# One hybrid encoder kernel: weight chunks split two ahead, index lookups in three queued parts, attention in steps of two heads of each group

## The chip, the cores and the metric

The kernel runs on one core of a Trainium2 chip, in one launch. The metric is the time of the launch on the device in microseconds (us); less is better. Engines: PE (TensorE, matrix multiply), PEld (its weight loads), DVE (VectorE), ACT (ScalarE), POOL (GpSimd), SP (SyncE, which issues most DMAs). Each engine works through its own queue in order and waits there for what an instruction needs.

## What is computed

Two layers over 512 tokens of width 1024. Each layer has a mixer (attention in windows, a short convolution and a pooling branch side by side) and a PEER block, a retrieval of 16384 one-neuron experts. Cut to what matters:

```python
for l in range(2):
    h = rms_norm(x, norm1_g[l]) * (1 + scale1) + shift1
    q, k, v, conv_x, conv_b, conv_c, pool_x = split(h @ w_in[l])
    attn = windowed_gqa(rope(norm(q)), rope(norm(k)), v, sink)   # 8 q heads, 2 kv heads, blocks of 128, +-128 tokens
    conv = conv_b * short_conv(conv_c * conv_x)                  # 256 channels
    pool = per_group_map(multiscale_pool(pool_x)) * pool_scale   # 256 channels, windows 2, 4, 8, 16
    x = x + gate1 * (concat(attn, conv, pool) @ w_out[l])
    h2 = rms_norm(x, norm2_g[l]) * (1 + scale2) + shift2
    # PEER: two scores of 128 keys per head, top 16 of each, top 16 of their 256 sums
    v1, i1 = top_k(q1 @ keys0.T, 16); v2, i2 = top_k(q2 @ keys1.T, 16)
    top, pos = top_k(v1[:, None] + v2[None, :], 16)
    e = (i1 * 128 + i2)[pos]; gate = softmax(top)                # 8 heads x 16 experts a token
    x = x + gate2 * sum_k(gate_k * gelu(h2 . peer_u[e_k]) * peer_v[e_k])
```

## The kernel before

Activations lie transposed in SBUF, 128 features on the partitions and 512 tokens along the row (`hh` and `hl`, a high and a low part, since f32 products are built from three matmuls of parts).

**The weight stream.** All large weights (w_in, w_out, peer_wq and the transposed peer_u) come as chunks of 128 x 1024. A chunk is loaded into `wr` by a DMA that SP issues (L251), its high part is cast into `wh` by ScalarE (`prep_hi`, L263), and the low part is the difference, `wl`, made by DVE or GpSimd (`prep_lo`, L272). `half` lists chunks with the high part alone, `ready` those with both. `chunk` (L295) takes a ready one, prepares one high and one low part for later chunks, and then queues the 24 matmuls of its own (L291 to L293: high x high, high x low, low x high). There are three `wh` and three `wl` buffers and five `wr`. In the steady state one chunk is ready and one half.

**do_A** (L816) is one such chunk of peer_u against 384 of the 512 tokens, then a gelu on ScalarE (L822) and, for the first AHEAD = 56 of the 128 chunks, a DMA of the result to `Sd` in DRAM (L824). These 56 stand in as PE work beside the selection; the rest follow in the dense stage.

**The selection and slots.** `scores` and `pairs` run DVE's max, index and replace operations for the top 16. `slots` (L1178) turns positions of the top 16 sums into two indices and the gates, some twenty DVE operations. `lookup` (L1212) picks the expert indices by these: ScalarE copies the indices out into `rep` (L1216), DVE compares (`soh`, L1218), multiplies by `rep` (L1220) and adds up (L1223, L1226). `operands` transposes the results on PE (L930), and ScalarE and DVE lay them out as `ij` and `gg`.

**The token loop** (`g8`, 48 groups of 8 tokens): DVE makes one-hot matrices `oh` for the next group (L949 to L952), PE multiplies them (L980, L981) into a matrix of gates over experts, ScalarE copies it to `stg` (L983), and every fourth group goes to `Gd` in DRAM. At groups 3 and 7 of each 16 a `lookup` for the next 128 tokens is queued whole. `fill` keeps two sums, of DVE's and of PE's work in us, and queues a do_A whenever PE's lags, up to do_A 51; the others follow behind the loop.

**The dense stage** runs over 128 expert blocks: load of peer_v, high and low part (`vh`, `vl`), weights from `Gd` and the gelu, 18 matmuls (`vmul`, L1033 to L1038), and for the last 128 tokens gathers by indirect DMA with DVE products.

**Attention** runs in eight steps (four blocks of 128 queries, two kv groups `g`). `att_scores` does four heads of one group: one f32 matmul each on 64 rows of `qk` (L674, two passes), masks by bf16 matmuls on 128 rows (L678), row maximum on DVE (L681), then exponentials on ScalarE (L692). `att_norm` scales, `att_turn` transposes on PE (L712), `att_out` multiplies by `v` (L721). On PE a step is: transposes of step i, scores of step i + 2, output of step i.

The order on each engine is the order in which the program issues; tile pools with a fixed number of buffers add the waits.

## Time and profile before

| | us |
|---|---|
| median of 3 runs (3032.3 to 3038.93) | 3036.97 |
| the profiled execution | 3036.9 |
| its span, first to last instruction | 3035.1 |
| PE busy in the span | 2904.2 (96%) |
| DVE busy | 2401.6 (79%) |
| ACT busy | 1265.9 (42%) |
| POOL busy | 918.0 (30%) |
| mean granted clock of PE | 0.977 |

Busy times of engines overlap and don't add up to the span. A busy PE is not PE at its peak: ends of matmuls are modelled, and a matmul at the lower clock counts as busy for longer. So the rows below give idle time, clock and waits by stage.

### The profile page before, as it was taken

The numbers are of one execution on the slowest core, as the hardware profiler recorded it, in microseconds if no ns is written. First come the engines' busy times: TensorE is split into PE (matmuls) and PEld (weight loads), VectorE is DVE, ScalarE is ACT, GpSimd is POOL, SyncE is SP. The second block draws the span as 40 slices with busy tenths as digits, with TensorE's granted clock in tenths as the row PEclk, the third lists the DMA queues.
The fourth block names the chain that finished last, engine by engine and source line by source line (L and its number), as shares of the span: only waits on it lengthen the run. The fifth ranks groups of instructions, "written<-read, shape, count | busy, mean of one in ns | idle before, by whom it ended". The sixth has DMA issues, their size and how long they took to land.

```text
span 3035.1 us, 41249 instructions
## 1 busy us (share of the span) xinstructions
PE 2904.2 (96%) x15116; PEld 2507.1 (83%) x15116; DVE 2401.6 (79%) x4617; ACT 1265.9 (42%) x1774; POOL 918.0 (30%) x782
## 2 busy tenths in 40 slices
PE   5999979999999999999999999799999999999999
PEld 3647879889888888888866678798988888888887
DVE  7966978776888888888868579778578888888887
ACT  4343346664333333333343343566633333333332
POOL 5405500002343343333333243000033333334342
PEclk7999989999999999999999999899999999999999
DMA  6524236569999999999943323465799999999996
GB/s 229 174 71 133 87 101 239 211 224 331 349 359 354 350 366 350 347 361 355 328 146 125 104 80 97 133 234 213 263 324 337 332 350 337 330 342 350 326 336 236
DMA packets 312971, 782.73 MB, mean 258 GB/s; under 512 B 26784, under 2 KB 154176, under 8 KB 309696
## 3 DMA queue, kind: packets, MB, share of 16 engines
q1 hardware_dynamic: 218992, 438.68, 42.7%
q0 software_dynamic: 73920, 268.53, 24.1%
q10 hardware_dynamic: 19856, 72.88, 6.2%
q8 instruction: 118, 1.93, 0.3%
q14 instruction: 85, 0.70, 0.1%
HBM read 705.02 MB, written 74.97 MB: 257 GB/s over the span
## 4 chain that ended last, share of the span: by engine, by line
PE 81%; DVE 14%; ACT 3%; issue 1%; POOL 0%; ACTq 0%; DMA 0%; DVEq 0%; POOLq 0%
PE pa L293 13%; PE pa L291 13%; PE pa L292 13%; PE pb L1034 6%; PE pb L1035 6%; PE pb L1038 6%; PE pb L1033 6%; PE pb L1037 6%; PE pb L1036 6%; PE pb L980 1%; PE pb L981 1%; PE pb L721 1%; PE pb L674 1%; DVE wl L272 1%; DVE I L1163 1%
## 5 line engine op out<-in xcount | busy, mean ns | idle before, releaser
L293 PE MATMUL pa<-hh,wl 128*128 128x384 f32 (+1 forms) x2568 | 906.9, 353 | 64.3 <-DVE wl L272 64.3
L291 PE MATMUL pa<-hh,wh 128*128 128x384 f32 (+1 forms) x2568 | 915.9, 357 | 28.1 <-ACT hh L364 24.5
L292 PE MATMUL pa<-hl,wh 128*128 128x384 f32 (+1 forms) x2568 | 903.8, 352 | 10.2 <-DVE hl L357 9.7
L293 PEld LDWEIGHTS pa<-hh,wl 128*128 128x128 f32 x2568 | 493.2, 192 | 91.1 <-DVE wl L272 69.9
L291 PEld LDWEIGHTS pa<-hh,wh 128*128 128x128 f32 x2568 | 493.9, 192 | 71.1 <-ACT hh L364 26.8
L1015 DVE TENSOR_TENSOR vl<-vr,vh 128x1024 fp32r<-128x1024 f32 x256 | 313.7, 1225 | 291.4 <-ACT vh L1014 277.4
L292 PEld LDWEIGHTS pa<-hl,wh 128*128 128x128 f32 x2568 | 492.9, 192 | 39.9 <-DVE hl L357 14.0
L1014 ACT CAST vh<-vr 128x1024 fp32r<-128x1024 f32 x256 | 269.5, 1053 | 504.0 <-PE pb L1038 266.3
L1051 POOL DMA_INDIRECT row<-in_peer_u_dram,eidx x256 | 307.8, 1202 | 541.7 <-DVE acc L1064 406.9
L1060 POOL DMA_INDIRECT row<-in_peer_v_dram,eidx x256 | 311.2, 1216 | 458.3 <-DVE row L1055 408.4
L272 DVE TENSOR_TENSOR wl<-wr,wh 128x1024 fp32r<-128x1024 f32 x265 | 323.5, 1228 | 82.2 <-ACT wh L263 79.2
L263 ACT CAST wh<-wr 128x1024 fp32r<-128x1024 f32 x331 | 348.8, 1055 | 75.6 <-PE pa L292 32.5
L1064 DVE SCALAR_TENSOR_TENSOR acc<-row,gw,acc 128x1024 f32<-128x1024 f32 x256 | 327.6, 1280 | 0.1
L822 ACT ACTIVATE ga<-pa 128x384 f32<-128x384 f32 x256 | 125.8, 492 | 466.7 <-PE pa L293 464.5
L1055 DVE SCALAR_TENSOR_TENSOR row<-row,htok 128x1024 f32<-128x1024 f32 x256 | 311.8, 1219 | 0.0
L1034 PE MATMUL pb<-vh,whi 128*128 128x512 f32 x768 | 300.7, 392 | 0.0
L1035 PE MATMUL pb<-vl,whi 128*128 128x512 f32 x768 | 300.5, 391 | 0.0
L1038 PE MATMUL pb<-vh,wlo 128*128 128x512 f32 x768 | 299.9, 391 | 0.0
L1037 PE MATMUL pb<-vh,wlo 128*128 128x512 f32 x768 | 299.3, 390 | 0.0
L1033 PE MATMUL pb<-vh,whi 128*128 128x512 f32 x768 | 299.0, 389 | 0.0
L1036 PE MATMUL pb<-vl,whi 128*128 128x512 f32 x768 | 298.5, 389 | 0.0
L272 POOL TENSOR_TENSOR wl<-wr,wh 128x1024 fp32r<-128x1024 f32 x66 | 170.0, 2587 | 198.1 <-ACT wh L263 198.1
(304 smaller groups left out, 3820.8 us busy)
## 6 DMA issues: line engine op xcount, KB each, us to landing
wr<-in_peer_uT_dram SPq DMA_DIRECT2D x256, 512.0 KB
vr<-in_peer_v_dram SPq DMA_DIRECT2D x256, 512.0 KB
Gd<-stg ACTq DMA_DIRECT2D x24, 2048.0 KB
adaw<-in_w_ada_dram SPq DMA_DIRECT2D x80, 512.0 KB
gtFalse<-Gd SPq DMA_DIRECT2D x36, 768.0 KB
Sd<-ga ACTq DMA_DIRECT2D x112, 192.0 KB
gtTrue<-Gd SPq DMA_DIRECT2D x28, 768.0 KB
gs<-Sd SPq DMA_DIRECT2D x112, 192.0 KB
```

The source lines that it names most:

```text
L263: self.nc.scalar.copy(hi, raw)
L272: (eng or self.nc.vector).tensor_tensor(lo, raw, hi.bitcast(F32), ALU.subtract)
L291: nc.tensor.matmul(ps[:, :width], wh, hh[c][:, :width], start=c == first, stop=False)
L292: nc.tensor.matmul(ps[:, :width], wh, hl[c][:, :width], start=False, stop=False)
L293: nc.tensor.matmul(ps[:, :width], wl, hh[c][:, :width], start=False, stop=c == last)
L1033: nc.tensor.matmul(y0, a, vh[:, 0:512], start=f, stop=False)
L1034: nc.tensor.matmul(y1, a, vh[:, 512:1024], start=f, stop=False)
L1035: nc.tensor.matmul(y0, a, vl[:, 0:512], start=False, stop=False)
L1036: nc.tensor.matmul(y1, a, vl[:, 512:1024], start=False, stop=False)
L1037: nc.tensor.matmul(y0, z, vh[:, 0:512], start=False, stop=e)
L1038: nc.tensor.matmul(y1, z, vh[:, 512:1024], start=False, stop=e)
L1064: nc.vector.scalar_tensor_tensor(acc, r, wb[bt - 1][:, k:k + 1], acc, ALU.mult, ALU.add)
```

## The change

Five edits:

1. `stream_init` gets `deep = 1`; `do_A` sets it to 2 for the first 56 chunks, and `chunk` then goes on preparing until two chunks are ready. `wh` has four buffers.
2. The pool branch writes its mean into a tile that it already has and the difference into `u`, so the two `pm` tiles are gone.
3. Attention steps take two heads of each group: four score matmuls alternate between rows 0 to 63 and 64 to 127 and come before all masks; the output is two matmuls of 256 columns per key block, one for each group.
4. `slots` is a generator that stops before its last part; a do_A is queued there.
5. `lookup` is a generator of three parts: `rep` on ScalarE; compare and multiply; the adds. In the token loop they are queued at groups 2, 3, 4 and 6, 7, 8, and `fill` is told 2.5 and 1.8 us instead of 5.5. `operands` still stands at group 11.

```diff
--- before.py
+++ after.py
@@ -244,6 +244,7 @@
         self.raws = []
+        self.deep = 1
@@ -259,7 +260,7 @@
         if hi is None:
-            hi = self.wp.tile([P, D], F32R, tag="wh", name=self.n("wh"), bufs=3)
+            hi = self.wp.tile([P, D], F32R, tag="wh", name=self.n("wh"), bufs=4)
@@ -296,6 +297,9 @@
         self.prep_lo(eng)
+        while self.deep > len(self.ready) and self.half:
+            self.prep_hi()
+            self.prep_lo(eng)
@@ -559,18 +563,18 @@
                 g.tensor_tensor(s4[:, 2:527], s2[:, 1:526], s2[:, 3:528], ALU.add)
-                dst = t([P, S], F32, "pm", bufs=2)
-                if c == 0:
-                    g.tensor_tensor(dst[0:64], s2[0:64, 8:520], self.icnt[0:64, 0], ALU.mult)
-                    g.tensor_tensor(dst[64:128], s4[64:128, 8:520], self.icnt[64:128, 0], ALU.mult)
-                else:
+                lo_, hi_ = s2, s4
+                if c:
...
                     g.tensor_tensor(s16[64:128, 8:520], s8[64:128, 4:516], s8[64:128, 12:524], ALU.add)
-                    g.tensor_tensor(dst[0:64], s8[0:64, 8:520], self.icnt[0:64, 1], ALU.mult)
-                    g.tensor_tensor(dst[64:128], s16[64:128, 8:520], self.icnt[64:128, 1], ALU.mult)
-                g.tensor_tensor(dst, dst, u[:, 8:520], ALU.subtract)
+                    lo_, hi_ = s8, s16
+                mean = hi_[:, 8:520]
+                g.tensor_tensor(mean[0:64], lo_[0:64, 8:520], self.icnt[0:64, c], ALU.mult)
+                g.tensor_tensor(mean[64:128], mean[64:128], self.icnt[64:128, c], ALU.mult)
+                dst = u[:, 8:520]
+                g.tensor_tensor(dst, mean, dst, ALU.subtract)
@@ -664,27 +668,28 @@
 
-            def att_scores(n_, g):
+            def att_scores(n_, jp):
                 k0, k1, w = span(n_)
-                pb = g * 64
                 mx = t([P, 4], F32, "mx", bufs=3)
-                sc = []
-                for j in range(4):
-                    b = bankB()
+                sc = [bankB() for _ in range(4)]
+
+                for i, b in enumerate(sc):
+                    j, pb = 2 * jp + i // 2, i % 2 * 64
...
                                      qk[pb:pb + 64, 0, k0 * P:k1 * P], start=True, stop=False)
-                    outer = [kb for kb in range(k0, k1) if kb != n_]
+                outer = [kb for kb in range(k0, k1) if kb != n_]
+                for i, b in enumerate(sc):
...
                                          start=False, stop=kb == outer[-1])
-                    nc.vector.tensor_reduce(mx[:, j:j + 1], b[:, :w], AX.X, ALU.max)
-                    sc.append(b)
+                    nc.vector.tensor_reduce(mx[:, i:i + 1], b[:, :w], AX.X, ALU.max)
+                two = lambda v_: v_.rearrange("p (j g) -> p j g", g=2)
                 nm = t([P, 4], F32, "nm", bufs=3)
-                sk = sinkb[:, g * 4:(g + 1) * 4]
-                nc.vector.scalar_tensor_tensor(nm, mx, 0.125, sk, ALU.mult, ALU.max)
+                sk = sinkb.rearrange("p (g j) -> p j g", g=2)[:, 2 * jp:2 * jp + 2]
+                nc.vector.scalar_tensor_tensor(two(nm), two(mx), 0.125, sk, ALU.mult, ALU.max)
                 es = t([P, 4], F32, "es", bufs=3)
-                nc.vector.tensor_tensor(es, sk, nm, ALU.subtract)
+                nc.vector.tensor_tensor(two(es), sk, two(nm), ALU.subtract)
@@ -704,7 +709,7 @@
 
-            def att_turn(n_, g, pr):
+            def att_turn(n_, pr):
@@ -715,13 +720,17 @@
 
-            def att_out(n_, g, pts, av):
-                k0, pb = span(n_)[0], g * 64
+            def att_out(n_, jp, pts, av):
+                k0 = span(n_)[0]
                 for kb, pt in enumerate(pts):
-                    nc.tensor.matmul(av[pb:pb + 64], v[:, k0 + kb, pb:pb + 64], pt,
-                                     start=kb == 0, stop=kb == len(pts) - 1)
-
-            order = [(n_, g) for n_ in range(4) for g in range(2)]
+                    pt4 = pt.rearrange("p (j g q) -> p j g q", j=2, g=2)
+                    for g in range(2):
+                        pb = g * 64
+                        nc.tensor.matmul(av[pb:pb + 64, jp * 256:(jp + 1) * 256].rearrange("p (j q) -> p j q", j=2),
+                                         v[:, k0 + kb, pb:pb + 64], pt4[:, :, g],
+                                         start=kb == 0, stop=kb == len(pts) - 1)
+
+            order = [(n_, jp) for n_ in range(4) for jp in range(2)]
@@ -734,8 +743,8 @@
             av, wo, pso, late = None, [], [], None
-            for idx, (n_, g) in enumerate(order):
-                pts = att_turn(n_, g, att.pop(idx)[0])
+            for idx, (n_, jp) in enumerate(order):
+                pts = att_turn(n_, att.pop(idx)[0])
@@ -747,11 +756,11 @@
                     self.mm(pso[-1], wo[-1], cat_h, cat_l, S, range(4, 8), 4, -1)
-                if g == 0:
+                if jp == 0:
                     av = bankC()
-                att_out(n_, g, pts, av)
+                att_out(n_, jp, pts, av)
                 bg(1)
-                if g == 1:
+                if jp == 1:
@@ -816,6 +825,7 @@
                 done[0] += 1
+                self.deep = 2 if i < AHEAD else 1
@@ -898,7 +908,10 @@
 
-                If, ab = self.slots(u, tu, I, gates, Pi)
+                sl = self.slots(u, tu, I, gates, Pi)
+                next(sl)
+                do_A()
+                If, ab = next(sl)
@@ -952,10 +965,15 @@
 
-                r0 = self.lookup(u, ab, If, 0, 0)
+                l0, l1 = (self.lookup(u, ab, If, 0, z) for z in range(2))
+                next(l0)
                 do_A()
-                r1 = self.lookup(u, ab, If, 0, 1)
+                next(l0)
+                r0 = next(l0)
+                next(l1)
                 do_A()
+                next(l1)
+                r1 = next(l1)
@@ -963,11 +981,17 @@
                     nxt = onehots(g8 * 8 + 8) if g8 + 1 < DT // 8 else None
-                    if z in (3, 7):
-                        ops[tt + 1, z] = self.lookup(u, ab, If, tt + 1, z // 4)
-                        fill(5.5)
+                    if z in (2, 6):
+                        look = self.lookup(u, ab, If, tt + 1, z // 4)
+                        next(look)
+                    elif z in (3, 7):
+                        next(look)
+                        fill(2.5)
+                    elif z in (4, 8):
+                        ops[tt + 1, z] = next(look)
+                        fill(1.8)
                     elif z == 11:
-                        late = operands(tt + 1, ops[tt + 1, 3], ops[tt + 1, 7])
+                        late = operands(tt + 1, ops[tt + 1, 4], ops[tt + 1, 8])
@@ -1199,6 +1223,7 @@
         nc.vector.scalar_tensor_tensor(w, a, 48.0, w, ALU.add, ALU.min)
+        yield
@@ -1207,24 +1232,26 @@
         nc.vector.tensor_tensor(e4, e4, sm.unsqueeze(2).broadcast_to([P, 4 * NH, TOPK]), ALU.mult)
-        return If, ab
+        yield If, ab
...
         nc.scalar.copy(rep, If[:, z, tt].unsqueeze(3).broadcast_to(shp))
+        yield
...
         nc.vector.tensor_tensor(oh, oh, rep, ALU.mult)
+        yield
...
         nc.vector.tensor_tensor(r.rearrange("p (h k) -> p h k", h=NH), oh[:, :, 0], oh[:, :, 1], ALU.add)
-        return r
+        yield r
...
```

In the rows of order below, lines are those of either kernel (wl is made in L272 before and in L273 after the change, the lookup in L1218 to L1226 and in L1244 to L1253, one-hots in L949 to L952 and in L962 to L965, scores and masks in L674, L678 and in L678, L683). Before the change DVE's queue reads so at the first lookup of the token loop of layer 0 (`soh`: the lookup's work tile; `wl`: low part of a weight chunk; `oh`, `oi`: one-hots of a group of tokens):

```order
L952 TENSOR_TENSOR oh_3643<-oi_3644,gg_3453 128x1024
L1218 TENSOR_TENSOR soh_3651<-iotaA,ab_3308 128x2048
L1220 TENSOR_TENSOR soh_3651<-soh_3651,rep_3649 128x2048
L1223 TENSOR_TENSOR soh_3651<-soh_3651 128x8x128
L1223 TENSOR_TENSOR soh_3651<-soh_3651 128x8x64
L1223 TENSOR_TENSOR soh_3651<-soh_3651 128x8x32
L1226 TENSOR_TENSOR sres_562_3657<-soh_3651 128x128
L272 TENSOR_TENSOR wl_3664<-wr_3610,wh_3612 128x1024
L272 TENSOR_TENSOR wl_3698<-wr_3660,wh_3662 128x1024
L949 TENSOR_TENSOR oh_3748<-iota,ij_3451 128x1024
L950 TENSOR_TENSOR oi_3749<-iota,ij_3451 128x1024
```

Both low parts stand behind the whole lookup. In the changed kernel the same place of DVE's queue reads so:

```order
L1244 TENSOR_TENSOR soh_3709<-iotaA,ab_3366 128x2048
L1246 TENSOR_TENSOR soh_3709<-soh_3709,rep_3647 128x2048
L273 TENSOR_TENSOR wl_3717<-wr_3670,wh_3672 128x1024
L962 TENSOR_TENSOR oh_3767<-iota,ij_3509 128x1024
L963 TENSOR_TENSOR oi_3768<-iota,ij_3509 128x1024
L964 TENSOR_TENSOR oh_3767<-oi_3768,gg_3511 128x1024
L965 TENSOR_TENSOR oh_3767<-oi_3768,gg_3511 128x1024
L1250 TENSOR_TENSOR soh_3709<-soh_3709 128x8x128
L1250 TENSOR_TENSOR soh_3709<-soh_3709 128x8x64
L1250 TENSOR_TENSOR soh_3709<-soh_3709 128x8x32
L1253 TENSOR_TENSOR sres_577_3776<-soh_3709 128x128
L273 TENSOR_TENSOR wl_3783<-wr_3713,wh_3715 128x1024
```

A low part and one set of one-hots now stand between the product with `rep` and the adds, and one low part behind the adds.

Before the change DVE's queue reads so from the end of `slots` to the first lookup in layer 0 (`f`, `ab`, `ge`: tiles of slots):

```order
L1201 SCALAR_TENSOR_TENSOR f_3293<-f_3293 128x512
L1203 CAST ab_3308<-f_3293 128x512
L1204 TENSOR_TENSOR ab_3308<-f_3293 128x512
L1207 TENSOR_REDUCE gsm_3311<-ge_1922 128x32
L1208 RECIPROCAL gsm_3311<-gsm_3311 128x32
L1209 TENSOR_TENSOR ge_1922<-ge_1922,gsm_3311 128x512
L1218 TENSOR_TENSOR soh_3327<-iotaA,ab_3308 128x2048
L1220 TENSOR_TENSOR soh_3327<-soh_3327,rep_3325 128x2048
```

No chunk is prepared between these. In the changed kernel the same place of DVE's queue reads so:

```order
L1225 SCALAR_TENSOR_TENSOR f_3317<-f_3317 128x512
L273 TENSOR_TENSOR wl_3337<-wr_3281,wh_3283 128x1024
L1228 CAST ab_3366<-f_3317 128x512
L1229 TENSOR_TENSOR ab_3366<-f_3317 128x512
L1232 TENSOR_REDUCE gsm_3369<-ge_1940 128x32
L1233 RECIPROCAL gsm_3369<-gsm_3369 128x32
L1234 TENSOR_TENSOR ge_1940<-ge_1940,gsm_3369 128x512
L273 TENSOR_TENSOR wl_3390<-wr_3333,wh_3335 128x1024
L1244 TENSOR_TENSOR soh_3419<-iotaA,ab_3366 128x2048
L1246 TENSOR_TENSOR soh_3419<-soh_3419,rep_3383 128x2048
```

Two low parts now stand here, one ahead of the last part of `slots` and one behind it.

Before the change PE's queue reads so in attention, at the scores of the second step of layer 0 (`pb`: a PSUM bank, one for each head; the first two heads of four):

```order
L674 MATMUL pb_1002<-qk_142 128x256
L678 LDWEIGHTS identb
L678 MATMUL pb_1002<-maskb,identb 128x128
L674 MATMUL pb_1006<-qk_142 128x256
L678 LDWEIGHTS identb
L678 MATMUL pb_1006<-maskb,identb 128x128
```

Each head's mask follows its score. In the changed kernel the same place of PE's queue reads so:

```order
L678 MATMUL pb_1000<-qk_142 128x256
L678 MATMUL pb_1001<-qk_142 128x256
L678 MATMUL pb_1002<-qk_142 128x256
L678 MATMUL pb_1003<-qk_142 128x256
L683 LDWEIGHTS identb
L683 MATMUL pb_1000<-maskb,identb 128x128
L683 LDWEIGHTS identb
L683 MATMUL pb_1001<-maskb,identb 128x128
```

The score matmuls of four heads now stand together, and all masks behind them.

## Rows read from the trace of the kernel before

**Rows 1.** Busy time by stage: start and end of the stretch and its length in us, then for each engine busy us and (number of instructions), the mean granted clock of PE, the DMA share and GB/s. The stretches are attention, head, token loop, tail and dense stage of layer 0, then attention, head and loop of layer 1.

```profile
143.80:217.50 73.70, 71.03 (x269) 34.51 (x268) 52.54 (x131) 31.74 (x98) 5.01 (x2) 0.93 0.26 80
...
368.70:432.30 63.60, 48.14 (x254) 47.24 (x253) 48.29 (x189) 25.70 (x31) 6.53 (x11) 0.87 0.35 106
432.30:682.40 250.10, 229.98 (x1759) 222.84 (x1759) 194.21 (x273) 164.53 (x186) 0.00 (x0) 0.95 0.60 213
682.40:711.70 29.30, 29.30 (x169) 29.00 (x168) 9.34 (x9) 14.66 (x19) 6.57 (x6) 1.00 0.87 326
711.70:1513.00 801.30, 801.30 (x3911) 711.35 (x3911) 676.39 (x893) 291.45 (x405) 305.98 (x251) 1.00 0.98 353
...
1643.40:1712.60 69.20, 66.39 (x269) 32.48 (x268) 52.48 (x132) 31.64 (x98) 5.04 (x2) 1.00 0.29 85
...
1863.80:1927.40 63.60, 48.09 (x254) 47.19 (x253) 48.34 (x189) 25.70 (x31) 6.53 (x11) 0.87 0.34 105
1927.40:2177.50 250.10, 230.06 (x1759) 222.91 (x1759) 194.24 (x273) 164.51 (x186) 0.00 (x0) 0.95 0.60 213
```

**Rows 2.** Timeline of ScalarE's queue in the tail: start us, duration us, the issue of the DMA that stores a chunk's gelu.

```profile
699.69 0.33 ACTq L824 DMA_DIRECT2D Sd<-ga  x1
...
703.85 0.33 ACTq L824 DMA_DIRECT2D Sd<-ga  x1
```

**Rows 3.** PE's waits in the whole span: tile and line that waited, engine, tile and line that it waited for, us in total, times, longest us.

```profile
PE pa L293 <- DVE wl L272: 64.3, 16, 8.5
...
PE pb L674 <- ACT pr L692: 2.4, 4, 1.0
...
PE pb L674 <- DVE qk L595: 1.5, 2, 0.8
```

**Rows 4.** DVE's waits in the token loop of layer 0 (432.3 to 682.4), same columns.

```profile
DVE wl L272 <- ACT wh L263: 20.3, 12, 2.8
DVE soh L1220 <- ACT rep L1216: 16.5, 6, 4.7
DVE oh L949 <- PE pb L981: 13.0, 9, 2.8
```

**Rows 5.** Timeline around the first lookup of the token loop of layer 0: start us, duration us, engine, line, operation, tiles, in brackets the idle time before it and what ended it.

```profile
448.35 0.49 ACT L822 ACTIVATE ga<-pa 128x384 f32<-128x384 f32 x1 [1.28 <-PE pa L293]
...
449.24 1.90 ACT L1216 COPY rep<-If 128x2048 f16<-128x2048 f16 x1 [0.40 <-ACT ga L822]
...
451.17 1.23 DVE L1220 TENSOR_TENSOR soh<-soh,rep 128x2048 f16<-128x2048 f16 x1 [4.73 <-ACT rep L1216]
...
454.15 2.35 DVE L272 TENSOR_TENSOR wl<-wr,wh 128x1024 fp32r<-128x1024 f32 x2
...
455.42 0.44 PE L293 MATMUL pa<-hh,wl 128*128 128x384 f32 x1 [2.60 <-DVE wl L272]
```

**Rows 6.** PE's waits for low parts in layer 0, first in the head (368.7 to 432.3), then in the token loop (432.3 to 682.4); columns as in rows 3.

```profile
PE pa L293 <- DVE wl L272: 13.7, 2, 8.5
...
PE pa L293 <- DVE wl L272: 18.4, 6, 3.5
```

**Rows 7.** DVE's waits in the head of layer 0 (368.7 to 432.3).

```profile
DVE wl L272 <- ACT wh L263: 7.4, 1, 7.4
DVE gg L938 <- ACT gg L936: 6.3, 1, 6.3
DVE soh L1220 <- ACT rep L1216: 0.7, 1, 0.7
```

**Rows 8.** Timeline of DVE in the head of layer 0, from the end of the selection to the second set of one-hots.

```profile
386.68 2.35 DVE L272 TENSOR_TENSOR wl<-wr,wh 128x1024 fp32r<-128x1024 f32 x2
...
399.32 0.69 DVE L1183 CAST If<-I 128x1024 f16<-128x1024 uint32 x1
...
409.50 1.22 DVE L1218 TENSOR_TENSOR soh<-iotaA,ab 128x2048 f16<-128x2048 f16 x1
...
428.54 0.69 DVE L938 SCALAR_TENSOR_TENSOR gg<-pb,gg 128x512 f16<-128x512 f32 x1 [6.34 <-ACT gg L936]
429.15 1.22 DVE L272 TENSOR_TENSOR wl<-wr,wh 128x1024 fp32r<-128x1024 f32 x1
430.29 0.68 DVE L949 TENSOR_TENSOR oh<-iota,ij 128x1024 f16<-128x1024 f16 x1
...
432.81 0.69 DVE L949 TENSOR_TENSOR oh<-iota,ij 128x1024 f16<-128x1024 f16 x1
```

**Rows 9.** Timeline of PE in attention of layer 1: the scores of one step on 384 keys, the output matmuls behind them (128 x 512, two passes for each of three key blocks) and the first transpose of the next step.

```profile
1678.91 0.91 PE L674 MATMUL pb<-qk 64*128 64x384 f32 x2
1679.75 0.28 PE L678 MATMUL pb<-maskb,identb 128*128 128x128 bf16 x2
1679.97 0.91 PE L674 MATMUL pb<-qk 64*128 64x384 f32 x2
...
1683.14 2.79 PE L721 MATMUL pb<-pt,v 128*64 128x512 f32 x6
1685.86 0.33 PE L712 MATMUL pa<-ident,pr 128*128 128x128 f32 x1
```

## Prediction

> **What bounds the kernel now.** The sum is made against the profiled execution, 3036.9 us with a span of 3035.1; the median of the three runs shown is 3036.97, so nothing has to be converted. I read the table by stage first. Both layers are alike to a few tenths of a microsecond in every stage from the top-16 selection to the dense loop, so I work on layer 0 and double [rows 1]. In the dense stage (711.7 to 1513) PE is busy in all of 801.3 us at clock 1.00: no other engine's work can move it. Time to be had lies ahead of it: the **head** (368.7 to 432.3, the first ten do_A chunks beside the end of the selection, slots and the first two lookups), where PE is idle for 63.6 - 48.1 = 15.5 us and the clock is 0.87; the **token loop** (432.3 to 682.4), idle 250.1 - 230.0 = 20.1 us, clock 0.95; and attention, busy almost throughout. The **tail** (682.4 to 711.7, seven chunks) has no idle time and full clock, and shows what a chunk costs: 4.16 us from one Sd store to the next [rows 2].
>
> The table of PE's waits names the cause: 64.3 us in 16 waits, eight a layer, are matmuls L293 that want wl, the low part of a weight chunk [rows 3]. DVE's own waits say why wl is late. In the loop DVE stands 16.5 us waiting for rep, which ScalarE copies, and 20.3 us for wh [rows 4]. One lookup shows it whole: ScalarE comes to rep at 449.24, because it had the gelu of a running chunk ahead of it; DVE's product waits 4.73 us for rep, does the lookup, and only then, at 454.15, the two wl behind it; PE gets the first at 455.42 [rows 5]. Six such lookups and two waits in the head (the selection's last part, then slots with the first lookup) are the eight waits [rows 6].
>
> The price is idle time plus clock. (1 - 0.87) x 63.6 = 8.3 us and (1 - 0.95) x 250.1 = 12.5 us are lost to the slow clock, a mix of its two levels: a mean of 0.87 is 26% of the time at 1.2 GHz and the rest at 2.4. Stages without idle time stand at 1.00, so I let the slow clock go with the waits; about 3 us of it falls into the idle time itself (idle share of each stage times its clock loss). All that could come back in a layer is 15.5 + 20.1 + 8.3 + 12.5 - 3 = 53.4 us.
>
> **Lookup in three parts and two ready chunks (counted together, since either covers most of the same waits).** The loop's DVE order now has a set of one-hots and a wl between the product and the reduction, and rep is asked for one token group earlier. A group takes PE about 250.1/48 = 5.2 us, more than the 4.73 us that DVE waited, so rep is there. Should DVE be late all the same, PE has a second ready wl, 4.16 us of work, against waits of at most 3.5 us in the loop [rows 6]. I take all loop waits on wl as gone. No instruction is added to DVE: the loop makes two chunks less (fill is told 4.3 us instead of 5.5 per lookup; its rule then gives 39 do_A instead of 41), one more is made ahead of it and one more in the tail.
> Loop: 250.1 - 20.1 - 12.5 + 1.0 (double counted) = 218.5; plus 1.7 for PE's wait for the second set of one-hots (DVE makes a set in 432.81 - 430.29 = 2.5 us, PE uses it up in about 1); less 2 x 4.16 = 211.9. DVE's work in it is 194.2 - 2 x 1.2 = 191.8, so PE bounds the loop, by 20 us.
> Head: DVE sets its end. From the end of the selection (386.68) to the first set of one-hots (432.81) pass 46.1 us, 7.4 + 0.7 + 6.3 = 14.4 of them waits [rows 7, 8]; 31.7 is work, and one wl more (429.15 to 430.29, 1.15) makes 32.8. Of the waits I leave 3: a cast behind the table load and exponential, and gg behind operands' transposes. One-hots are then ready at 386.7 + 32.8 + 3 = 422.5 instead of 432.35, 9.8 earlier. PE has by then only 368.7 + 11 x 4.16 + about 1.5 for the score and operand matmuls = 416, so some **6 us of idle time stay in the head**, and with them, I estimate, 2 us of slow clock (between 0 and 6, the latter being what the head loses now less the part in its idle time).
> Tail: 29.3 + 4.16 = 33.5.
> Sum: end of the tail 422.5 + 211.9 + 33.5 = 667.9 instead of 711.7, less 2 for the clock: 41.8 a layer, **84 us in all**. The bounds are 51 a layer (53.4 less the 1.7) and 25 (rival (c)).
>
> **What carries the depth.** A fourth wh (4 KB a partition) is paid for by the dropped pm tiles: the pool branch issues the same POOL instructions onto tiles that already live, nothing. wl keeps three buffers, so with two ready and one in use DVE's next wl waits for the chunk before. Behind it on DVE stand the one-hots. In the loop that is harmless: it is PE being behind. In the dense stage nothing takes the depth back, so the wait stays there, but DVE has a stricter one beside it: vl of the next step (two buffers) waits for the vmul that PE does after that chunk. I cost it at nothing. The two chunks of the head that use POOL give it a third wl, 2.4 us on an engine with nothing else then. Layer 1's mixer starts with one high part more in hand; it comes back to the old state at the two takes in attention.
>
> **slots with a do_A inside.** It puts one wl (1.15 us) into the DVE chain of the head, counted above, and 4.16 us of PE work into what was an 8.5 us wait [rows 6].
>
> **Attention.** A group of four heads is 1678.91 to 1683.14 = 4.23 us on PE: a pair of score matmuls 0.84, two masks 0.22, four times over [rows 9]. The 512-column matmuls behind it take (1685.86 - 1683.14)/6 = 0.45, so 384 columns stream in 0.34 and a pair in 0.68; 0.16 of the 0.84 is load and turning, which now falls due once in a group, and so does the way back from the masks (I take 0.1 of the 0.22). New group: 4 x 0.68 + 0.16 + 8 x 0.06 + 0.1 = 3.46, 0.77 less. Two of eight groups wait for exponentials and not for PE (L674 on pr, [rows 3]); six groups are 4.6. The first group no longer needs the last rotary step (0.8, half of 1.5 in two layers, [rows 3]), but its maxima are behind that on DVE: nothing. Output matmuls are twice as many at half the width: the same. I take 4.5 us a layer, **9 in all**, with 0 and 8 a layer as ends: 8 is half of the 69.2 - 52.5 = 16.7 us by which DVE is idle there [rows 1], since the reductions now start after four heads and not after one.
> The turn between 64 and 128 rows shows as the 0.16 us. The Trainium skill, page "TensorEngine Tiling (Array Packing)", section "Key Properties", says that a change of tiling mode drains the engine, which agrees, and that tiles on different rows can load and multiply at the same time, which no row here can show, since neighbours are now on the same rows. By that rule the pairs of the two groups would run side by side; the rival below has its result. The same page, section "PSUM Bottleneck", says that reading the results out does not get faster by it.
>
> **Rivals.**
> (a) The pairs of heads run side by side. Scores and output then take half of their 0.68 and 0.45; PE falls under DVE, whose 52.5 us plus its waits hold the stage at about 8 less a layer: 3037 - 84 - 16 = 2937. For: the order on PE allows it. Against: each pair is two passes on the same rows, so only every second neighbour differs.
> (b) Attention gives nothing, because reductions start later and exponentials hold the banks: 2953. For: the L674 waits on pr. Against: there are few of them, 2.4 us.
> (c) DVE becomes the loop's bound: its 191.8 us plus the waits for wh and rep that it has now, 20.3 + 16.5, would be 229 instead of 212, so 2944 + 2 x 17 = 2978 [rows 4]. For: 92% load. Against: both waits come from ScalarE being behind a running chunk, and both are asked for earlier now.
> (d) The depth is not there: three wl buffers and one DVE queue bring the second wl no sooner. Then the split lookup works alone, the loop's waits go by it, and the head keeps its first wait, 13.7 - 8.5 = 5.2 us on PE [rows 6]: 2944 + 2 x 5 = 2954.
> (e) Slower: the wl that waits for PE holds up DVE in the dense stage after all, in front of vl and the gather's products. It has to cost 93/144 = 0.65 us at each of the 144 chunks there to eat the gain; at 1 us it is 2944 + 144 = 3088. For: DVE works 676 of 801 us there. Against: the stricter vl, and PE waits for nothing there now.
>
> **How the numbers follow.** Forecast 3036.9 - 84 - 9 = 2944, chance 0.62; (a) 0.10, (b) 0.12, (c) 0.07, (d) 0.05, (e) 0.02, something without effect 0.02. The forecast's own terms reach from 2 x 51 + 16 = 118 less (2919) to 2 x 25 = 50 less (2987); not all ends fall together, and 2926 to 2968 holds the forecast's middle, (a), (b) and (d), eight in ten. What a measurement of this kernel can tell from no change is about 0.2%, 6 us. Faster by more 0.96, within 0.02, slower by more 0.02.
>
> **What would show it.** Right: PE's waits for wl fall from 64.3 to under 10 us; DVE's waits for rep vanish; the loop is near 212 us at clock 0.99 or more; the first one-hot matmul comes about 10 us after less work on DVE, with some 6 us of PE waits before it; attention near 65 us in layer 1; the dense stage 801 us as before. Wrong: DVE waits for wl's buffer followed by PE waits for one-hots; a dense stage over 805 us; L674 waits for pr that eat the shorter groups; a slow clock that stays in the loop.

## The result, and the profile after

The changed kernel takes **2922.63 us** (median of 4 runs, 2921.94 to 2925.92), the kernel before, on the same chip, 3037.74 us. The ratio is 0.9627, 95% interval 0.961 to 0.9643: about 115 us less, where 93 were forecast. It lies 3.4 us below the low end of the range. The profiled execution has a span of 2920.3 us, 114.8 less than before.

The table by stage of the kernel after, columns as in [rows 1]: attention, head, loop, tail and dense stage of layer 0, then attention, head and loop of layer 1.

```profile
144.20:203.60 59.40, 53.70 (x309) 34.53 (x308) 50.37 (x130) 32.35 (x99) 4.65 (x2) 0.91 0.31 92
...
354.90:407.80 52.90, 49.26 (x279) 48.48 (x278) 49.54 (x190) 27.58 (x33) 8.88 (x12) 0.97 0.49 152
407.80:618.30 210.50, 208.89 (x1709) 203.25 (x1709) 189.87 (x271) 163.98 (x183) 0.00 (x0) 1.00 0.69 246
618.30:651.80 33.50, 33.50 (x199) 33.50 (x197) 11.28 (x11) 15.33 (x19) 6.01 (x6) 1.00 0.98 359
651.80:1470.10 818.30, 818.30 (x3987) 725.44 (x3986) 687.74 (x907) 297.25 (x413) 305.61 (x251) 1.00 0.96 345
1581.90:1643.90 62.00, 52.38 (x309) 33.76 (x308) 53.04 (x131) 31.40 (x98) 3.85 (x2) 0.94 0.30 98
...
1795.20:1848.00 52.80, 49.16 (x278) 48.38 (x277) 49.57 (x190) 27.52 (x32) 8.84 (x12) 0.97 0.50 152
1848.00:2058.40 210.40, 208.93 (x1709) 203.28 (x1709) 189.80 (x271) 163.91 (x183) 0.00 (x0) 1.00 0.69 246
```

Against [rows 1]: the loop lost its 20 us of idle time and all of its slow clock, and PE fills 208.9 of 210.5 us. The head still has 3.6 us without PE work and clock 0.97. The dense stage is PE's throughout, as before (818.3 us here, cut at its last vmul; cut so, it was 818.4). Attention is another stage than it was: PE, busy in 66.4 of 69.2 us of layer 1 before, is busy in 52.4 of 62.0, no more than DVE.

PE's waits in the whole span, kernel after, columns as in [rows 3].

```profile
PE pb L678 <- ACT pr L697: 10.7, 12, 2.1
...
PE pb L943 <- DVE sres L1253: 5.1, 2, 2.5
...
PE pa L294 <- DVE wl L273: 2.2, 2, 1.1
PE pb L678 <- DVE tmp L597: 2.1, 1, 2.1
...
PE pb L1004 <- DVE oh L964: 1.9, 2, 0.9
```

The waits for wl (L294 here, L293 before) fell from 64.3 us to 2.2, and scores waiting for exponentials rose from 2.4 to 10.7 us: the new wait is in attention. The wait for `sres`, 2.5 us a layer, is that of `operands` for the lookup's result in the head. DVE's waits in the loop of layer 0, to be read beside [rows 4]: rep is there in time now, wh is not always, and the ready chunks cover that.

```profile
DVE wl L273 <- ACT wh L264: 14.9, 13, 3.7
...
DVE soh L1246 <- ACT rep L1241: 0.5, 1, 0.5
```

One attention step on 384 keys, timeline of the kernel after (columns as in [rows 5]).

```profile
176.55 0.58 ACT L697 ACTIVATE pr<-pb,nm 128x384 f32<-128x384 f32 x1 [2.12 <-DVE nm L693]
...
177.27 2.60 PE L678 MATMUL pb<-qk 64*128 64x384 f32 x8 [1.13 <-ACT pr L697]
...
179.80 0.62 PE L683 MATMUL pb<-maskb,identb 128*128 128x128 bf16 x8
180.12 1.95 DVE L686 TENSOR_REDUCE mx<-pb 128x1 f32<-128x384 f32 x4
...
180.35 1.52 PE L729 MATMUL pb<-pt,v 128*64 128x256 f32 x12
...
182.50 0.17 DVE L693 TENSOR_SCALAR nm<-nm 128x4 f32<-128x4 f32 x1
...
182.76 0.58 ACT L697 ACTIVATE pr<-pb,nm 128x384 f32<-128x384 f32 x1 [2.14 <-DVE nm L693]
```

From the first score to the first output matmul pass 177.27 to 180.35 = 3.08 us (4.23 before, 3.46 forecast, both between the same two points), and the output takes 1.52 us as twelve passes of half width, where six of full width took 2.79 [rows 9]. One exponential to the same one of the next step is 6.21 us.

Lengths of the stages in the traces, layer 0 / layer 1, in us. Attention is from the first score to the end of the last output matmul, head from the first do_A chunk to the first one-hot matmul, loop to the last one-hot matmul, tail to the first vmul. The last column is the ratio of the run's time to that of the kernel before, which was run beside it on the same chip each time (medians of 3035.9 to 3037.7 us).

| kernel | attention | head | loop | tail | time | ratio (95%) |
|---|---|---|---|---|---|---|
| before | 72.9 / 68.4 | 63.6 / 63.6 | 249.8 / 249.8 | 29.5 | 3037.7 | |
| after | 59.5 / 61.9 | 52.8 / 52.8 | 210.6 / 210.4 | 33.5 | 2922.6 | 0.9627 (0.961 to 0.9643) |
| e1_no_att | 69.6 / 75.5 | 52.6 / 52.6 | 212.2 / 212.0 | 33.5 | 2949.7 | 0.9716 (0.9699 to 0.9733) |
| e2_att_only | 59.3 / 59.7 | 63.2 / 63.3 | 249.7 / 249.7 | 29.5 | 3012.8 | 0.9922 (0.9905 to 0.9938) |
| e3_no_deep | 59.3 / 59.8 | 59.0 / 59.0 | 212.2 / 212.2 | 33.7 | 2936.7 | 0.9673 (0.9657 to 0.969) |
| e4_no_split | 59.3 / 61.9 | 53.2 / 54.0 | 221.4 / 220.3 | 29.3 | 2937.1 | 0.9673 (0.9657 to 0.9689) |
| e13_slots_only | 59.2 / 61.4 | 63.8 / 63.6 | 240.6 / 242.3 | 29.5 | 3000.4 | 0.9882 (0.9864 to 0.9901) |
| e5_rows | 60.4 / 61.0 | 52.8 / 52.6 | 210.5 / 212.3 | 33.5 | 2926.8 | 0.9639 (0.9622 to 0.9655) |
| e6_cols | 59.6 / 62.3 | 52.6 / 52.8 | 212.0 / 210.6 | 33.5 | 2925.7 | 0.9636 (0.962 to 0.9652) |
| e10_out_wide | 61.5 / 63.5 | 52.9 / 52.8 | 210.6 / 210.6 | 33.5 | 2928.7 | 0.9642 (0.9625 to 0.9659) |
| e7_mask_pair | 59.2 / 61.8 | 52.8 / 52.8 | 210.5 / 210.6 | 33.5 | 2923.9 | 0.9629 (0.9613 to 0.9645) |
| e9_both | 59.9 / 61.9 | 52.8 / 52.8 | 210.4 / 210.5 | 33.5 | 2926.1 | 0.964 (0.9624 to 0.9656) |
| e11_free | 58.2 / 59.4 | 52.6 / 52.8 | 212.2 / 210.5 | 33.5 | 2922.7 | 0.9626 (0.9609 to 0.9644) |
| e12_head12 | 59.3 / 61.9 | 54.6 / 54.5 | 212.6 / 212.0 | 29.3 | 2923.3 | 0.9626 (0.9608 to 0.9644) |

The intervals are about 5 us to either side. So runs that differ by less are told apart by their stages alone, and those of attention, head and loop move by 1.7 us and more with where a stretch at the lower clock falls (below).

### The profile page after: what moved, and what is told of

The parts are those of the page before. It is cut to its first block, busy times and chain, and to the rows that moved or that the text cites. A ratio compares the mean times of both kernels' runs of the same rounds, so it can differ in the third digit from the quotient of the medians.

```text
span 2920.3 us, 41477 instructions
## 1 busy us (share of the span) xinstructions
PE 2840.1 (97%) x15196; PEld 2479.3 (85%) x15196; DVE 2399.2 (82%) x4616; ACT 1267.5 (43%) x1774; POOL 911.5 (31%) x783
## 4 chain that ended last, share of the span: by engine, by line
PE 81%; DVE 16%; ACT 1%; issue 1%; POOL 0%; DMA 0%; DVEq 0%; ACTq 0%; POOLq 0%
PE pa L292 13%; PE pa L294 13%; PE pa L293 13%; PE pb L1058 6%; PE pb L1059 6%; PE pb L1062 6%; PE pb L1061 6%; PE pb L1057 6%; PE pb L1060 6%; PE pb L1004 1%; PE pb L1005 1%; DVE I L1187 1%; DVE s L1183 1%; DVE I L1181 1%; DVE mx L686 1%
## 5 line engine op out<-in xcount | busy, mean ns | idle before, releaser
L292 PE MATMUL pa<-hh,wh 128*128 128x384 f32 (+1 forms) x2568 | 904.7, 352 | 28.0 <-ACT hh L368 24.4
L293 PE MATMUL pa<-hl,wh 128*128 128x384 f32 (+1 forms) x2568 | 892.3, 347 | 10.9 <-DVE hl L361 10.3
L294 PE MATMUL pa<-hh,wl 128*128 128x384 f32 (+1 forms) x2568 | 892.7, 348 | 2.2 <-DVE wl L273 2.2
L292 PEld LDWEIGHTS pa<-hh,wh 128*128 128x128 f32 x2568 | 484.4, 189 | 70.0 <-ACT hh L368 26.7
L293 PEld LDWEIGHTS pa<-hl,wh 128*128 128x128 f32 x2568 | 484.4, 189 | 40.2 <-DVE hl L361 14.4
L294 PEld LDWEIGHTS pa<-hh,wl 128*128 128x128 f32 x2568 | 483.8, 188 | 23.9 <-DVE wl L273 2.8
L273 DVE TENSOR_TENSOR wl<-wr,wh 128x1024 fp32r<-128x1024 f32 x264 | 324.0, 1228 | 67.7 <-ACT wh L264 33.7
L264 ACT CAST wh<-wr 128x1024 fp32r<-128x1024 f32 x331 | 349.0, 1056 | 44.2 <-DMA wr<-in_peer_uT_dram 21.5
L1007 ACT ACTIVATE stg<-pb 128x512 f32<-128x512 f32 x192 | 198.3, 1162 | 33.3 <-PE pb L1005 27.6
```

The lines of the kernel that those rows point to most:

```text
L264: self.nc.scalar.copy(hi, raw)
L273: (eng or self.nc.vector).tensor_tensor(lo, raw, hi.bitcast(F32), ALU.subtract)
L292: nc.tensor.matmul(ps[:, :width], wh, hh[c][:, :width], start=c == first, stop=False)
L293: nc.tensor.matmul(ps[:, :width], wh, hl[c][:, :width], start=False, stop=False)
L294: nc.tensor.matmul(ps[:, :width], wl, hh[c][:, :width], start=False, stop=c == last)
```

## Experiments: the parts

**e1_no_att and e2_att_only**: the changed kernel with the old attention, and the old kernel with the new attention.

```diff
 (e1: att_scores to att_out and their loop as before; e2: only these as changed)
-            def att_scores(n_, jp):
+            def att_scores(n_, g):
```

> The changed kernel with attention as it was before (steps of four heads of one group); all else as changed. Theory (the stage table of the two traces): attention is worth 13.4 us in layer 0 and 6.5 us in layer 1, 19.9 us in all, and nothing behind it depends on it, so 2922.6 + 20 = 2942.5 us (2938 to 2946), attention back at about 73 and 68 us, head, loop and tail unchanged at 52.8, 210.5 and 33.5 us. Rival (the forecast's own term): the attention edit is worth 9 us and the remaining 11 us come from how the parts meet, so 2931.6 us. Second rival: the half clock in layer 0's attention (147 to 151 and 168 to 175 us in the kernel before) was luck of that run, and attention is worth 2 x 6.5 = 13 us: 2935.6 us.

> The kernel before with the new attention steps alone. Theory: 3037.7 - 20 = 3017.8 us (3014 to 3022), attention at about 59.5 and 62 us, head, loop and tail as before (63.6, 249.8, 29.5 us). Rival (the forecast's term of 9 us): 3028.7 us. If the parts are independent, the gain here and the loss without the attention edit are equal, and the rest of the change is worth 115 - 20 = 95 us.

Attention is worth 27 us by the first (2949.7 against 2922.6) and 23 us by the second (3012.8 against 3035.9 for the kernel before beside it), not 9, and rather more than the 20 of the two traces; both runs lie outside what was expected of them (2938 to 2946 and 3014 to 3022 us), on the side of a larger gain. The rows of e1 give a reason for the difference (table by stage, attention of layer 0 and of layer 1):

```profile
143.80:213.40 69.60, 67.68 (x269) 33.49 (x268) 51.78 (x130) 32.58 (x99) 4.95 (x2) 0.98 0.27 84
1595.90:1671.40 75.50, 72.39 (x269) 34.88 (x268) 54.77 (x131) 31.73 (x98) 3.81 (x2) 0.91 0.27 84
```

The old attention is PE's: with clock 1.00 it takes 68.4 us (layer 1, [rows 1]), with 0.98 it takes 69.6, with 0.93 72.9 and with 0.91 75.5. The new one takes 59.5 us in layer 0 at 0.91, and 59.6 at 0.97 in the same place of e6 (below): PE's clock is not its bound. The rival that counted the slow clock as luck, with 13 us for attention, is refuted too: the new attention takes away the exposure to it.

**e3_no_deep and e4_no_split**: one ready chunk, lookups and slots divided; two ready chunks, lookups and slots whole.

```diff
-                self.deep = 2 if i < AHEAD else 1
+                self.deep = 1
 (e4; the lookups of the head are queued whole, too)
                 next(sl)
-                do_A()
                 If, ab = next(sl)
...
-                    if z in (2, 6): ... elif z in (4, 8): ... fill(1.8)
+                    if z in (3, 7):
+                        look = self.lookup(u, ab, If, tt + 1, z // 4)
+                        next(look); next(look); ops[tt + 1, z + 1] = next(look)
+                        fill(5.5)
```

> The changed kernel with one chunk ready instead of two (deep stays 1); lookups and slots stay divided. Theory (either part covers most of the waits): the loop's waits are gone by the divided lookup, and the head has one wait back, 13.7 - 8.5 = 5.2 us a layer by the kernel before, less some of it because do_A now stands inside slots: 2 to 5 us a layer, 2927 to 2933 us; loop at 211 to 213 us. Rival: the depth carries the change, PE waits for wl come back at the lookups and with them the slow clock, 15 us a layer or more: over 2952 us. Second rival: the depth brings nothing at all, 2922.6 us within 2 us.

> The changed kernel with lookups and slots queued whole as before (at groups 3 and 7, fill told 5.5 us), the depth of two stays. Theory (either part covers most of the waits): two ready chunks are 8.3 us of work against waits of 3.5 us in the loop and 8.5 us in the head, so few us a layer: 2926 to 2934 us. Rival: DVE still stands for rep (16.5 us a layer before) and for wh (20.3 us), and 194 us of work plus 16.5 to 37 us of waits make DVE the loop's bound: loop 211 to 231 us and, with two chunks more in the loop and no do_A in slots, up to 20 us a layer: about 2945 to 2963 us, with PE waits for one-hots in place of those for wl.

Each costs 14 us, and the times lie 4 and 3 us above the ranges of their theories; the forecast's rival (d) had 10 for the missing depth. The loop without depth is 212.2 us, as far from 210.5 as one stretch at the lower clock, and the head has its wait back: PE's waits of e3 in head, loop and tail of layer 0,

```profile
PE pa L294 <- DVE wl L273: 7.0, 4, 5.2
```

one of 5.2 us among them, 19 us behind the head's start as in the kernel before: the 13.7 - 8.5 of the forecast. Without the division DVE still stands for rep, 14.0 us in the loop (its waits in e4, 407 to 632):

```profile
DVE soh L1242 <- ACT rep L1237: 14.0, 6, 3.0
DVE wl L273 <- ACT wh L264: 6.9, 10, 1.0
```

but PE waits for wl only twice in head and loop together, 3.2 us: two ready chunks cover it. The loop is 10 to 11 us longer; 8.3 of them are two chunks more, of which one comes off the tail (4.2 us). Neither rival with DVE as the bound came true.

**e13_slots_only**: of the change, the new attention and the do_A inside slots (the fourth `wh` buffer and the pool branch stay as changed, too; neither was tried by itself).

```diff
                 next(sl)
+                do_A()
                 If, ab = next(sl)
 (lookups whole, fill 5.5, deep = 1)
```

> Of the change only the new attention steps and the do_A inside slots: one chunk ready, lookups queued whole, fill told 5.5 us. The new attention alone measured 3012.8 us. Theory: PE's wait of 8.5 us at slots gets a chunk of 4.2 us, for which DVE pays one wl of 1.15 us: 2 to 3 us a layer less, 3006 to 3010 us; the loop stays at 249.7 us with its six waits for wl. Rival (with one chunk ready the do_A there lacks its wl too): 3012 to 3015 us. Either way depth and lookups together hold the rest of the gain, 84 to 90 us, of which each alone (2936.7 and 2937.1 us) brings all but 14.

12 us less than the new attention alone, twice the expectation. The head is as long as before with eleven chunks instead of ten, and the loop is shorter by 9.2 and 7.5 us for one chunk (4.16 us) less: head and loop of layer 0 in e13,

```profile
354.70:418.50 63.80, 51.59 (x278) 50.37 (x278) 49.43 (x190) 27.21 (x33) 6.49 (x11) 0.92 0.38 116
418.50:659.10 240.60, 220.64 (x1733) 213.33 (x1733) 192.51 (x272) 162.35 (x183) 0.00 (x0) 0.97 0.61 217
```

the other 3 to 5 us are clock: 0.97 and 0.96 in the two layers instead of 0.95, while the idle time is the 20 us that it was. With PE work in an idle stretch of the head, the clock behind it was higher as well. So, taken in this order, the parts are: attention 23, slots 12, depth and divided lookups together 78. Division and slots without depth (e3) bring all of the last two but 14, and so does depth without division and slots (e4).

## Experiments: attention

**e5_rows, e6_cols, e10_out_wide**: scores not in turn; output of one group first; output over all 128 columns.

```diff
 (e5)
-                for i, b in enumerate(sc):
-                    j, pb = 2 * jp + i // 2, i % 2 * 64
+                for i in (0, 2, 1, 3):
+                    b, j, pb = sc[i], 2 * jp + i // 2, i % 2 * 64
 (e6: for g outside of for kb; e10)
-                        nc.tensor.matmul(av[pb:pb + 64, ...], v[:, k0 + kb, pb:pb + 64], pt4[:, :, g], ...
+                        nc.tensor.matmul(av[:, ...], v[:, k0 + kb, :], pt4[:, :, g], ...
```

> The changed kernel with its four score matmuls of a step in the order rows 0, rows 0, rows 64, rows 64 instead of in turn; masks, output and all else as changed. Theory (neighbours on different rows overlap): a pair that follows another on the same rows takes 0.68 to 0.84 us as before, one that follows on other rows 0.56 us; with one turn in three instead of three, a score group takes 2.60 + 2 x 0.15 to 2 x 0.28 = 2.9 to 3.2 us instead of 2.6. The wait for exponentials hides part; if it hides none, 8 to 16 groups make up to 7 us: 2922.6 to 2930 us. Rival (grouping alone, fewer turns of the array, is what shortened the group, by 0.16 + 0.5 us): the group stays at 2.6 us.

> The changed kernel with the output matmuls of one group's key blocks first and then the other's, instead of in turn; all else as changed. Theory (neighbours that write different columns of the array run side by side): 12 passes of 256 columns take 1.45 us in the changed kernel and 2.6 to 2.8 us here, as the 6 passes of 512 columns did before (2.79 us); of the 1.2 us of a step, with PE waiting for exponentials in most steps, between 0 and 1.2 show in the time: 16 steps, 2922.6 to 2940 us. Rival: the half width alone made them shorter (each pass 0.22 us): the 12 passes take 1.45 to 1.6 us here too.

> The changed kernel whose output matmuls multiply by all 128 columns of v (both groups' heads into the same rows of the result, added up) instead of 64, so that two neighbours can't stand side by side in the array; count, length and order of the matmuls as changed. It changes the attention output: rows of one group get the other's sums too. Theory (the forecast's mis-sized term is the output, whose two halves run side by side): 12 passes take 12 x 0.216 = 2.6 us instead of 1.45, 8 passes 1.73 instead of 1.05; a layer has four steps of each, 4 x 1.15 + 4 x 0.7 = 7.4 us, of which PE's waits for exponentials (0.4 to 1.5 us a step) hide up to half: 8 to 15 us, 2930 to 2938 us. Rival (attention is held by exponentials and maxima, and PE's share in the output was of no matter): 2922 to 2926 us.

Timeline of the eight score passes of a step in e5,

```profile
164.38 2.68 PE L678 MATMUL pb<-qk 64*128 64x384 f32 x8 [0.93 <-ACT pr L697]
```

and of the twelve output passes of a step in e6 and in e10:

```profile
179.87 2.00 PE L729 MATMUL pb<-pt,v 128*64 128x256 f32 x12
```

```profile
181.69 2.81 PE L728 MATMUL pb<-pt,v 128*128 128x256 f32 x12
```

e10 shows that the output's halves run side by side in the changed kernel: over all columns twelve passes take 2.81 us, one behind the other, as long as the six of full width did; over 64 columns 1.52. In e6 they take 2.00, so the order matters, though less than expected: part of the second group's passes still falls beside the first's (in its last steps two passes begin 0.01 us apart). e10's time, 2928.7 us, lies between its theory's range and its rival's. Its attention is 2.0 and 1.6 us longer, far from 7.4, and its traces show where: from the first exponential of the last step to the end of attention it takes 11.2 us in both layers, the kernel after 9.0, and the way from the first exponential of all to that one is no longer (44.0 and 45.2 us, for 44.2 and 45.8). Ahead of it the output's gain lies under PE's waits. In e5 the scores take 2.68 us, against 2.60 in turn, and not the 2.9 to 3.2 expected. That does not settle whether scores run side by side: in the kernel after, the next bank comes every 0.56 us, an exponential's time, and four of them pace the group either way. It is settled where banks are free, in e9 below (timeline, two halves of one step's scores):

```profile
163.50 1.47 PE L680 MATMUL pb<-qk 64*128 64x384 f32 x4 [0.41 <-ACT pr L699]
...
165.23 0.92 PE L680 MATMUL pb<-qk 64*128 64x384 f32 x4
```

The second half, four passes, takes 0.92 us, no more than two passes on the same rows did (0.91, [rows 9]). The Trainium skill, page "TensorEngine Tiling (Array Packing)", section "Key Properties", says that different tiles can load weights and multiply in parallel; these rows agree with it.

**e7_mask_pair, e9_both, e11_free**: what holds attention now.

```diff
 (e7: masks and maxima behind each two scores; e9: e7 and)
-                    if j < 2:
+                    if j < 1:
                         nc.vector.tensor_scalar(pr[:, j, :w], pr[:, j, :w], sm[:, j:j + 1], None, ALU.mult)
-                        nc.vector.tensor_copy(dst, av4)
+                        nc.scalar.copy(dst, av4)
 (e11: e9 and)
-                nc.vector.scalar_tensor_tensor(two(nm), two(mx), 0.125, sk, ALU.mult, ALU.max)
+                nc.vector.scalar_tensor_tensor(two(nm), sk, 0.125, sk, ALU.mult, ALU.max)
```

> The changed kernel with masks and maxima behind each two score matmuls instead of behind all four. Theory (the step is a ring: exponentials free the banks, scores, masks, maxima, nm, exponentials again, 6.21 us at 176.55 to 182.76 us of the changed kernel's trace, and DVE is busy in 5.95 us of it): the ring gets about 1 us shorter but DVE's work now holds it, so at most 0.25 us a step: 2919 to 2923 us. Rival (the ring alone is the bound): 1 us less in each of some 12 steps: 2911 us. Second rival (one more turn of the array a step costs 0.3 us on PE): 2923 to 2928 us.

> As the kernel with masks behind each two score matmuls, and DVE relieved: three of the four scalings of a step on ScalarE instead of two (0.375 us off DVE, 0.56 us on ScalarE), the cast of the output (0.68 us in every second step) on ScalarE too. Theory (ring and DVE bound attention together): both are 0.7 to 1 us shorter a step, 12 to 14 steps: 2909 to 2914 us, attention near 54 and 56 us. Rival (ScalarE, 4.3 of 6.2 us busy and on the ring, becomes the bound): no gain, 2920 to 2926 us.

> As the kernel with masks behind each two scores and DVE relieved (2926.1 us, attention 59.9 and 61.9 us), but nm is made from the sinks alone and not from the maxima, which are still taken; the exponentials' scale is a small constant to keep them finite, so the attention output is another. It tells what holds attention now. Theory (the ring: exponentials, sum, scalings ahead of the maxima on DVE, maxima, nm, next exponentials, 5.9 us at 176.08 to 181.95 us of that kernel's trace): without the way from the maxima to the exponentials the step falls to DVE's work, 46.3 us of 59.9 in layer 0, or to PE's, about 48 without its waits: attention 50 to 54 us, 2908 to 2914 us. Rival (the work of an engine, not the ring, holds it, or the exponentials wait for DVE for other reasons): no more than 2 us less a layer, 2922 to 2926 us.

e7 brought no gain, as its theory had it (2923.9 us for 2919 to 2923; its time alone can't be told from the second rival's 2923 to 2928): its step from 178.03 to 184.23 us takes 6.20 us, 6.21 in the kernel after. e9 was to bring 8 to 14 us and brought none, although DVE has 4 us less to do a layer (46.3 instead of 50.4 us in layer 0). A step of e9, timeline:

```profile
176.08 0.58 ACT L699 ACTIVATE pr<-pb,nm 128x384 f32<-128x384 f32 x1 [1.29 <-PE pa L719]
...
178.32 0.21 ACT L701 ACTIVATE es<-es 128x4 f32<-128x4 f32 x1
...
178.57 0.16 DVE L706 TENSOR_TENSOR sm<-sm,es 128x4 f32<-128x4 f32 x1
...
179.31 1.94 DVE L688 TENSOR_REDUCE mx<-pb 128x1 f32<-128x384 f32 x4
...
181.69 0.17 DVE L695 TENSOR_SCALAR nm<-nm 128x4 f32<-128x4 f32 x1
...
181.95 0.58 ACT L699 ACTIVATE pr<-pb,nm 128x384 f32<-128x384 f32 x1 [1.28 <-DVE nm L695]
```

The maxima of the next group are queued on DVE behind the sums and scalings of this one, and these wait for all four exponentials. Earlier masks are of no use to a maximum that stands there. With less work on DVE, e9's step above is shorter, 5.87 us against 6.21. The step ahead of it, in which an output is cast, got longer: 7.43 us (168.65 to 176.08), 7.19 in the kernel after. The cast that went to ScalarE is now what DVE waits for, ahead of those sums (DVE's waits in e9, 163 to 197):

```profile
DVE hl L771 <- ACT hh L770: 3.8, 3, 1.4
```

That is nearly all that DVE was relieved of, so e9 does not show that less work on DVE would be worth nothing. In the middle of the stage (160 to 200 us) DVE is busy in 37.9 of 40 us in the kernel after and in 34.0 in e9. In e11, which has the same wait, attention is 1.7 and 2.5 us shorter than in e9, not 8. But that run does not decide: nm no longer reads the maxima and is still queued behind them, so the way round was cut in the data and not in the order. That PE does not hold the step is shown (10.7 us of its waits are for exponentials; e10 and e7 change PE's part and move attention by 2 us or nothing). Which of DVE's work, DVE's order and ScalarE's work would be next is open.

## Experiment: the head's idle time

**e12_head12**: one chunk more ahead of operands.

```diff
                 r1 = next(l1)
                 do_A()
+                do_A()
                 operands(0, r0, r1)()
```

> The changed kernel with one do_A more in the head, ahead of the operands of the first token group, and so one less in the tail. Theory (PE stands idle 2.7 us there, waiting for the transposes' input, and 3.6 us in the whole head, while DVE sets its end): the head gets 1.2 to 1.5 us longer, the wl of that chunk on DVE, the tail 4.2 us shorter: 2.7 us a layer, 2917 us (2915 to 2919). Rival (the chunk pushes transposes, gg and one-hots back by its whole 4.2 us): no gain, 2922 to 2925 us.

Head +1.8 and tail -4.2 us a layer, near the theory, and still no gain (2923.3 us): the loop is 1.6 to 2.0 us longer, and in this run so are, by 1.6 us each, the stretches ahead of attention, which the edit does not touch. Table by stretches of 1 us in the head of the kernel after (columns as in [rows 1]; PE's busy time is the first number behind the comma, its clock the third from the end):

```profile
399.00:400.00 1.00, 0.19 (x2) 0.00 (x0) 0.97 (x2) 0.60 (x2) 0.00 (x0) 1.00 0.54 147
400.00:401.00 1.00, 0.00 (x0) 0.00 (x0) 0.97 (x2) 0.00 (x0) 0.00 (x0) 1.00 0.93 368
401.00:402.00 1.00, 0.27 (x3) 0.27 (x3) 0.93 (x4) 0.00 (x0) 0.00 (x0) 0.96 0.80 292
402.00:403.00 1.00, 1.00 (x5) 1.00 (x4) 0.81 (x1) 0.68 (x1) 0.00 (x0) 0.50 0.03 8
...
405.00:406.00 1.00, 1.00 (x6) 1.00 (x5) 1.00 (x2) 0.00 (x0) 0.00 (x0) 0.83 0.81 332
406.00:407.00 1.00, 1.00 (x8) 1.00 (x7) 0.96 (x3) 0.00 (x0) 0.00 (x0) 1.00 0.38 66
```

and at the border of head and loop in e12:

```profile
409.00:410.00 1.00, 0.23 (x2) 0.10 (x1) 1.00 (x3) 0.49 (x1) 0.00 (x0) 1.00 0.43 173
410.00:411.00 1.00, 0.00 (x0) 0.00 (x0) 0.96 (x3) 0.00 (x0) 0.00 (x0) 1.00 1.38 142
411.00:412.00 1.00, 0.61 (x6) 0.49 (x6) 1.00 (x2) 0.00 (x0) 0.00 (x0) 0.79 0.55 186
412.00:413.00 1.00, 1.00 (x12) 1.00 (x11) 0.96 (x3) 0.45 (x1) 0.00 (x0) 0.50 0.91 357
```

PE idles 2.5 us for operands in the one and 2.1 us for one-hots in the other, and behind it the clock stands at the lower of its two levels, 1.2 GHz. So e12 has the idle stretch of the head no more, and the slow clock in the loop (0.98 and 0.99 for 1.00) instead of the head (1.00 for 0.97), in both layers. That the chunk moved it is not shown. In layer 0 of e6, whose head is that of the kernel after, PE idles as long at the same place, and the clock falls only behind the next idle stretch:

```profile
400.00:401.00 1.00, 0.00 (x0) 0.00 (x0) 0.93 (x3) 0.00 (x0) 0.00 (x0) 1.00 1.00 394
...
402.00:403.00 1.00, 1.00 (x8) 1.00 (x7) 0.72 (x1) 0.89 (x1) 0.00 (x0) 1.00 0.03 8
...
410.00:411.00 1.00, 0.66 (x6) 0.50 (x6) 1.00 (x2) 0.60 (x1) 0.00 (x0) 0.50 0.00 0
```

e6 then has a head of 52.6 us and a loop of 212.0, and one layer each of e5 and e11 has the same. So a slow stretch costs 0.2 us in the head, where DVE sets the end, and 1.4 to 1.8 in the loop, where PE does; what decides between the two places is open.

## Why the forecast was too high

The span fell by 114.8 us: 92.1 in head, loop and tail, 19.9 in attention, 1.4 in the selection, 1.3 ahead of attention. So of some 22 us that the forecast lacked, 11 are attention's and 8 to 9 are of head, loop and tail.

- **The term that failed is attention**: 9 forecast, 20 in the traces, 23 to 27 by the runs. e10, whose output costs PE what it did before, splits the 19.9 us of the traces in three. "Output matmuls are twice as many at half the width: the same" is wrong: they run side by side (1.52 us for 2.79; e10). At the end this is worth only 2.0 and 1.6 us a layer, 3.6 in all, as PE waits for exponentials. Next, layer 0's attention stood at clock 0.93 in [rows 1], although the forecast says that stages without idle time stand at 1.00; the sum took slow clock from head and loop and left it out here. That is 72.9 - 68.4 = 4.5 us, gone because PE no longer bounds the stage. What is left, 11.8 us, is between the kernel before and e10 (11.4 - 4.5 and 4.9 us) and belongs to the regrouped steps, for which 9 were forecast: near in size, but not by the forecast's sum of pairs one behind the other.
- **Rival (a) came true in its mechanism.** Score pairs and outputs run side by side, PE falls to DVE's level (52.4 and 53.0 us busy in layer 1), and PE waits for exponentials, which wait for DVE's nm. The forecast gave it a chance of 0.10. Its 16 us for both layers are near the 6.5 to 9 a layer that the new steps show against 68.4. "Each pair is two passes on the same rows", the reason against it, did not matter. The Trainium skill, page "TensorEngine Tiling (Array Packing)", section "PSUM Bottleneck", says that tiling does not speed up reading the results out; the traces agree, since an exponential that reads a bank takes 0.58 us in the kernel after (at 176.55 us, above) and took 0.58 us in the kernel before (at 181.20 us).
- **Head, loop and tail: 46.1 a layer for 41.8.** The loop came at 210.5 for 211.9 and the tail at 33.5 as worked out. The first one-hot comes 10.8 us earlier for 9.8. The 2 us taken off for slow clock were not due: the head's clock is 0.97, but its end is set by DVE, for which PE still waits 0.3 us at the first one-hots, so the slow stretch costs it 0.2 us (e12 above), and 3.6 us of idle time are left in it, not 6. Here the mechanism was right and the size too small.
- **Right:** the waits named by [rows 3] to [rows 6] were the cause; either of depth and division covers most of them (14 of some 90 us are lacking without depth, and 14 without division and slots); wl behind PE in the dense stage costs nothing (818.3 us with and without); DVE does not become the loop's bound, at 189.9 of 210.5 us.
- **Missed in e13:** the do_A in slots was counted as a wl on DVE and a chunk of PE; alone it also came with 3 to 5 us less of slow clock in the loop.

The forecast of rival (a), 2937, less the 4.5 us of slow clock in attention, 8.6 in head, loop and tail and 2.7 elsewhere, is 2921, near the 2922.6 measured. This sum was made from the measured stages and sums them up; it is no test.

## What to carry to other kernels

When work on one engine is cut, look at its slow stretches too: attention, once it left PE with spare time, no longer paid for a slow clock, and the old one, which PE bounds, paid all of it. Two measures that hide the same wait must be costed together, by taking one away at a time. And before shortening a step, follow it once round, from an exponential to the same one of the next step: earlier masks did nothing, since the queue order put the maxima behind sums that wait for all exponentials, and a cast taken off DVE came back as DVE's wait for that cast.
